# The second feed-forward block as two passes over DRAM instead of one fused loop per half of the tokens

## The chip, the cores and the metric

The kernel runs on one core of one Trainium2 chip. The metric is the device time of one execution in microseconds. Three runs of the kernel before took 2210.45, 2212.99 and 2214.95 us; the median is 2212.99 us.

## The reference

One inference step of a one-layer trunk, over 1104 columns of tokens (16 meta tokens, 1024 prompt tokens, 64 sample tokens), with 1024 features and 2816 hidden features, in fp32:

```
x = x + 0.5 * SwiGLU_1(RMSNorm(x))
x = x + W_out @ concat[RG-LRU, mLSTM, GLA](W_in @ RMSNorm(x))
x = x + 0.5 * SwiGLU_2(RMSNorm(x))
y = RMSNorm_final(x)            # the meta tokens are dropped here

def swiglu(x, w1, w3, w2):
    return (silu(x @ w1) * (x @ w3)) @ w2
```

The change lies in the third line and the last one: SwiGLU_2 on the 1088 columns that are put out (the meta tokens' 16 are not needed there), and the final norm.

## The kernel before

Tokens lie along the free dimension and features along the partitions (128 at a time, so D = 8 blocks and the hidden layer 22, `NFB`). Every fp32 product is made of three matmuls of a reduced type: `split` (L111) casts a tensor to its high part on ScalarE and subtracts that on VectorE to get the low part, and PE then sums hi·hi, hi·lo and lo·hi. So each weight that comes from DRAM costs ScalarE a cast and VectorE a subtraction (`whi`, `wlo`) before PE can use it.

The products with w1 and w3 are made of half-size blocks by a scheme with seven products in place of eight (`seven`, L1400): the weights' four blocks are combined on GpSimd (`ws`, L1384, four operations for each 256 features) into seven left operands, the normalized tokens' four blocks on VectorE into seven right operands `op1` to `op7` (L1344), each split; then 7 x 12 matmuls of half the part's width, and VectorE and ScalarE add the partial results from PSUM into `c` (L1416, L1420, L1424).

The second feed-forward block (L1270 to L1608) works on two parts of the tokens, `PARTS`: 576 columns (half width 288) and 512 columns (half width 256). For each part it goes through eleven groups of 256 hidden features (`f0`), and for each group does all of this:

- `weights` for w1 (two loads of 512 KB, four combinations, seven splits), `seven`, and the same for w3;
- `halves` (L1434): two loads of 512 KB of w2, each split (`w2h`, `w2l`);
- the gate (L1579 to L1581: tanh on ScalarE, two VectorE operations) and a split of its result (`hh`, `hl`);
- `gemm2` (L1525): 8 blocks of outputs, each 6 matmuls into PSUM per column block, which VectorE adds into the residual `X` (L1538), at every group.

w1, w3 and w2 are so loaded and prepared once for each part, which is 44 calls of `weights` and 44 halves of w2. The operands of part 1 are made while part 0 runs: squares at group 4, `norms` at 6, the normalization spread over groups 8 to 14, and the split operands in part 0's last group, into the buffers of part 0. The unnormalized part 1 waits in DRAM meanwhile (`xback`) and is loaded again. The outputs of part 0 (transposition of 4 blocks at a time into PSUM, L1451, a copy by ScalarE, squares, `rsq`, scaling, store) are spread over part 1's groups 4 to 12. The last group of part 1 has a form of its own (L1588 to L1603): its columns are transposed ahead, the w2 products are made with tokens on the partitions, and each chunk of 128 tokens is normed and stored as soon as it is summed.

Ahead of all this stands `wout2` (L1486): the last third of the mixer's output projection, eight blocks of 24 matmuls, interleaved with the squares, the norm and the operands of part 0.

The order of the instructions on each engine comes from a list scheduler of the framework: the program's order with priorities, and `tc.high_priority` around part 0's preparation. Loads and stores are issued by SP's queue, in that queue's order.

Names: `wraw` is a raw w1, w3 or w_out tile, `w` a raw w2 tile, `rb` the broadcast norm factor, `acc` and `sq` the squares, `rsv`, `rsa`, `rsy` the small tiles of the reciprocal square root, `xt` an output tile, `xps` its PSUM tile.

Of the kernel before, what the change touches and what calls it, by code (L numbers as in the profile page):

```python
# [30 lines left out]
PARTS = [(288, [(0, 64), (64, 128), (192, 128), (320, 128), (448, 128)]), (256, [(0, 128), (128, 128), (256, 128), (384, 128)])]  # L31
# [5 lines left out]
def tile_step(ctx, tc, A, O):  # L37
# [1233 lines left out]
    with ExitStack() as ph:  # L1271

        def pool(name, bufs=1, **kw):
            return ph.enter_context(tc.tile_pool(name=name, bufs=bufs, reuse_waits="tile", **kw))

        xp, wq, op_, tp, bp = pool("x3"), pool("w3"), pool("o3"), pool("t3", 2), pool("b3", 2)
        pq, pz = pool("q3", 2, space=PSUM), pool("z3", 2, space=PSUM)

# [6 lines left out]


        X = [xp.tile([128, 8, 2 * n], F32, tag=f"x{i}", name=f"x{i}") for i, (n, _) in enumerate(PARTS)]
        xback = tc.dram_tile([128, 8, 512], F32, name="xback")

        def load0():  # L1290
            nc.sync.dma_start(X[0][:, :, 0:320], xdr2[0][:, :, 16:336])
            nc.sync.dma_start(X[0][:, :, 320:576], xdr2[1][:, :, 0:256])


        def squares(i):
            n = PARTS[i][0]
            acc = tp.tile([128, 576], F32, tag="acc", name="acc", bufs=1)[:, : 2 * n]
            S.activation(acc, X[i][:, 0, :], AF.Square)
            for k in range(1, 8):
                q = tp.tile([128, 576], F32, tag="h", name="sq", bufs=3)[:, : 2 * n]  # L1300
                S.activation(q, X[i][:, k, :], AF.Square)
                V.tensor_tensor(acc, acc, q, OP.add)
            return acc

        def norms(i, acc):
            n = PARTS[i][0]
            r = tp.tile([128, 2, 288], F32, tag="rb", name="rb", bufs=1)[:, :, :n]
# [12 lines left out]
            for h in range(2):  # L1320
                q = pz_("rbp")
                for j, (hh, o, m) in enumerate(cs):
                    if hh == h:
                        d = tp.tile([128, 128], F32, tag="dg", name="dg", bufs=3)
# [6 lines left out]
        def normal(i, r, ks):  # L1331
            n = PARTS[i][0]
            for k in ks:
# [5 lines left out]
        def blocks(i):  # L1339
            n = PARTS[i][0]  # L1340
            return [X[i][:, 4 * fh : 4 * fh + 4, th * n : th * n + n] for fh, th in ((0, 0), (0, 1), (1, 0), (1, 1))]

        def minus(out, x, y):
            V.tensor_tensor(out, x, y, OP.subtract)  # L1344

        def temp(i):
            return bp.tile([128, 4, 288], F32, tag="bf", name="bf")[:, :, : PARTS[i][0]]

        def differences(i):
            b11, b12, b21, b22 = blocks(i)  # L1350
            t1, t2 = temp(i), temp(i)
            minus(t1, b12, b11)
            minus(t2, b22, t1)
            minus(b12, b22, b12)
            return t1, t2

        def operands(i, ts):
            n = PARTS[i][0]
            b11, t3, b21, b22 = blocks(i)
            t1, t2 = ts  # L1360
            ops = {}
            for p, x in zip(ORDER, (b11, t2, b21, t3, t1, t2, b22)):
                if p == 4:
                    minus(t2, b21, t2)
                t = op_.tile([128, 2, 4, 288], F32R, tag=f"op{p}", name=f"op{p}")
                ops[p] = (t[:, 0, :, :n], t[:, 1, :, :n])
                split(*ops[p], x)
            return ops
# [3 lines left out]
        def weights(w, f):  # L1372
            r = []
            for i in range(2):
                t = wq.tile([128, 4, 256], F32, tag="raw", name="wraw", bufs=4)
# [24 lines left out]
        def seven(u, ops, n, y1, y2):  # L1400
            a, b, c = bank("a"), bank("b"), bank("c")
            s = tp.tile([128, 288], F32, tag="p1", name="p1")[:, :n]
# [31 lines left out]
        def halves(f0):  # L1434
            wr = A["ffn2_w2"][f0 * 128 : f0 * 128 + 256, :].rearrange("(g p) (i c) -> i p g c", g=2, i=2)
            out = []
            for i in range(2):
                raw = lp.tile([128, 2, 512], F32, tag="w2", name="w2", bufs=1)
                lo = lp.tile([128, 2, 512], F32R, tag="w2l", name="w2l", bufs=2)
                hi = lp.tile([128, 2, 512], F32R, tag="w2h", name="w2h", bufs=2)  # L1440
                nc.sync.dma_start(raw, wr[i])
                split(hi, lo, raw)
                out.append((hi, lo))
            return out


        def turned(x, i, o, m):
            for q in range(2):
                p = pz_("xps").rearrange("p (k t) -> p k t", k=4)
                for k in range(4):  # L1450
                    PE.transpose(p[:m, k, :], X[i][:, 4 * q + k, o : o + m], ident)  # L1451
                S.copy(x[:m, q * 512 : q * 512 + 512].rearrange("p (k t) -> p k t", k=4), p[:m])

        def output(i, j, o, m, x, add=None):
            ahead = add is not None
            ss = tp.tile([128, 2], F32, tag="ssf", name="ssf", bufs=RB)[:m]
            v = tp.tile([128, 8], F32, tag="rsv", name="rsv", bufs=RB)[:m, :1]
            for q in range(2):
                xq = x[:m, q * 512 : q * 512 + 512]
                if add:  # L1460
                    add(q, xq)
# [199 lines left out]
```

## Time and profile before

| | before |
|---|---|
| median of three runs | 2212.99 us |
| the profiled execution: its time | 2212.36 us |
| its span (first to last instruction) | 2210.6 us |
| PE busy | 2112.8 us, 96%, 13758 matmuls |
| VectorE (DVE) busy | 1533.3 us, 69% |
| ScalarE (ACT) busy | 846.7 us, 38% |
| GpSimd (POOL) busy | 342.7 us, 16% |
| DMA | 195.90 MB, mean 89 GB/s |

The span is what the trace covers; the execution's time is 1.8 us longer, for what lies around it. Every later row is read against the span. A matmul's record overlaps the next one's, so PE's pace is read from the starts of successive matmuls, not from their durations. The granted clock of PE over the whole execution is 0.985 of full speed.

### The profile page before, as it was taken

Reading aid. Unit: us, or ns where it says so; the run is one execution under the profiler, and the core shown is the slowest. Engines: PE = TensorE matmul, PEld = TensorE weight load, DVE = VectorE, ACT = ScalarE, POOL = GpSimd, SP = SyncE. Lnnn points to the kernel's source line nnn. Section 1 sums busy time; section 2 is a strip of 40 time slices with the busy share of each in tenths; the row PEclk is TensorE's granted clock in tenths of the full one; section 3 lists DMA queues with packets and bytes.
Section 4 is the critical chain, followed back from the end, with each engine's and each line's share of the span. In section 5 each row is a group of like instructions: output and inputs, shape, how many; then the busy total and the mean of one; then the engine's idle time right before and its main releaser. Section 6 shows DMA issues by size and latency. Waiting matters only on the chain.

```text
span 2210.6 us, 35427 instructions
## 1 busy us (share of the span) xinstructions
PE 2112.8 (96%) x13758; PEld 2032.8 (92%) x13758; DVE 1533.3 (69%) x3214; ACT 846.7 (38%) x1672; POOL 342.7 (16%) x321
## 2 busy tenths in 40 slices
PE   8999999999999999999998897799999989999997
PEld 7999999999999999978997797799999989888896
DVE  7444545454444467766787885998978798779896
ACT  6221111111111144645646753444434344435543
POOL 3000000000000021000000000343333233234331
PEclk9999999999999999999999999999999999999999
DMA  6011111111111125544434337533233233233421
GB/s 180 29 48 39 53 34 48 48 48 39 48 48 39 39 73 152 131 141 132 111 100 105 87 101 211 173 90 96 77 89 93 86 115 92 90 101 96 124 87 48
DMA packets 237500, 195.90 MB, mean 89 GB/s; under 512 B 41887, under 2 KB 216516, under 8 KB 236820
## 3 DMA queue, kind: packets, MB, share of 16 engines
q1 hardware_dynamic: 232540, 191.86, 29.5%
q10 hardware_dynamic: 4792, 1.78, 0.4%
q8 instruction: 108, 1.77, 0.3%
q14 instruction: 60, 0.49, 0.1%
HBM read 162.28 MB, written 31.32 MB: 88 GB/s over the span
## 4 chain that ended last, share of the span: by engine, by line
PE 77%; DVE 13%; DMA 4%; ACT 3%; issue 2%; SPq 0%; DVEq 0%; ACTq 0%
PE p L196 24%; PE p L245 11%; PE p L1535 9%; PE pw L196 8%; PE b L1409 7%; PE c L1409 4%; PE a L1409 4%; DVE wlo L113 3%; PE pwo L196 2%; PE pA L752 1%; DVE c L1416 1%; PE pq L550 1%; DMA wraw<-in_w_out_dram 1%; DVE sl L134 1%; DVE h L1580 1%
## 5 line engine op out<-in xcount | busy, mean ns | idle before, releaser
L112 ACT CAST whi<-wraw 128x512 fp32r<-128x512 f32 (+1 forms) x242 | 189.7, 787 | 338.0 <-PE p L245 116.4
L113 DVE TENSOR_TENSOR wlo<-wraw,whi 128x512 fp32r<-128x512 f32 (+1 forms) x242 | 242.6, 1004 | 32.4 <-ACT whi L112 28.6
L247 DVE SCALAR_TENSOR_TENSOR x<-p,x 128x384 f32<-128x384 f32 (+1 forms) x264 | 139.6, 539 | 153.7 <-PE p L245 153.1
L196 PE MATMUL p<-sh,whi 128*128 128x384 f32 (+1 forms) x1056 | 205.0, 331 | 0.4 <-ACT sh L133 0.4
L196 PE MATMUL p<-sl,whi 128*128 128x384 f32 (+1 forms) x1056 | 203.2, 329 | 0.0
L196 PE MATMUL p<-sh,wlo 128*128 128x384 f32 (+1 forms) x1056 | 201.9, 329 | 0.0
L112 ACT CAST whi<-ws 128x512 fp32r<-128x512 f32 x176 | 108.9, 620 | 193.2 <-PE b L1409 117.9
L1384 POOL TENSOR_TENSOR ws<-wraw 128x512 f32<-128x512 f32 x88 | 137.5, 1563 | 290.3 <-DVE wlo L113 197.0
L196 PEld LDWEIGHTS p<-sh,whi 128*128 128x128 f32 x1056 | 179.4, 189 | 1.6 <-ACT sh L133 1.4
L196 PEld LDWEIGHTS p<-sh,wlo 128*128 128x128 f32 x1056 | 180.7, 188 | 0.0
L196 PEld LDWEIGHTS p<-sl,whi 128*128 128x128 f32 x1056 | 179.7, 188 | 0.1
L112 ACT CAST hh<-h 128x384 fp32r<-128x384 f32 (+3 forms) x110 | 61.5, 559 | 302.3 <-DVE h L229 278.2
L245 PE MATMUL p<-hh,whi 128*128 128x384 f32 (+1 forms) x528 | 174.3, 330 | 1.9 <-DVE x L247 1.8
L1535 PE MATMUL p<-hh,w2h 128*128 128x288 f32 (+1 forms) x512 | 166.1, 332 | 10.0 <-DVE x L1538 9.7
L1409 PE MATMUL b<-op,whi 128*128 128x288 f32 (+1 forms) x1056 | 164.5, 293 | 11.5 <-DVE c L1416 9.7
L1538 DVE SCALAR_TENSOR_TENSOR x<-p,x 128x288 f32<-128x288 f32 (+1 forms) x256 | 131.2, 523 | 62.8 <-PE p L1535 61.9
L245 PE MATMUL p<-hh,wlo 128*128 128x384 f32 (+1 forms) x528 | 174.1, 330 | 0.0
L245 PE MATMUL p<-hl,whi 128*128 128x384 f32 (+1 forms) x528 | 173.5, 329 | 0.0
L1535 PE MATMUL p<-hl,w2h 128*128 128x288 f32 (+1 forms) x512 | 168.1, 329 | 0.6 <-DVE hl L113 0.6
L1535 PE MATMUL p<-hh,w2l 128*128 128x288 f32 (+1 forms) x512 | 167.6, 328 | 0.0
L1409 PEld LDWEIGHTS b<-op,whi 128*128 128x128 f32 x1056 | 147.5, 192 | 15.7 <-DVE c L1416 12.0
L148 POOL TENSOR_TENSOR acc<-acc,sq 128x384 f32<-128x384 f32 (+1 forms) x21 | 22.8, 1085 | 773.7 <-ACT sq L147 773.1
(467 smaller groups left out, 4570.3 us busy)
## 6 DMA issues: line engine op xcount, KB each, us to landing
wraw<-in_ffn_w_dram SPq DMA_DIRECT2D x154, 512.0 KB
w<-in_ffn_w_dram SPq DMA_DIRECT2D x44, 512.0 KB
wraw<-in_w_in_dram SPq DMA_DIRECT2D x16, 512.0 KB
wraw<-in_w_out_dram SPq DMA_DIRECT2D x16, 512.0 KB
out_y_prompt_dram<-xt SPq DMA_DIRECT2D x16, 256.0 KB
xspill<-x SPq DMA_DIRECT2D x2, 1536.0 KB
sl<-in_x_prompt_dram SPq DMA_DIRECT2D x5, 512.0 KB
x<-xspill SPq DMA_DIRECT2D x2, 1280.0 KB
```

The lines of the kernel that those rows point to most:

```text
L112: S.copy(hi, x)
L113: V.tensor_tensor(lo, x, hi.bitcast(F32), OP.subtract)
L134: V.scalar_tensor_tensor(lo[:, k, :n], X[:, k, :n], vc(gname, k), hi[:, k, :n].bitcast(F32), OP.mult, OP.subtract)
L148: G.tensor_tensor(sums[b], sums[b], s, OP.add)
L196: PE.matmul(p, wsl(ww, k), xsl(xx, k), start=i == 0, stop=i == tot - 1)
L245: PE.matmul(p[:, :n], w[:, g, :], x[:, :n], start=i == 0, stop=i == 3 * GRP - 1)
L247: V.scalar_tensor_tensor(X[b][:, d, :n], p[:, :n], 0.25, X[b][:, d, :n], OP.mult, OP.add)
L550: PE.matmul(p[:96, h, :m], wt[:, kb, sl, 0:96], cm[:, kb, :m], start=i == 0, stop=i == len(ks) - 1)
L1384: G.tensor_tensor(t, x, y, op)
L1409: PE.matmul(t[:, :n], ww[:, k, :], xx[:, k, :], start=first and i == 0, stop=i == 11, skip_group_check=True,)
L1535: PE.matmul(p[:, :m], w[:, g, :], x, start=c == 0, stop=c == 5)
L1538: V.scalar_tensor_tensor(xs, p[:, :m], 0.25, xs, OP.mult, OP.add)
```

## The change

The second feed-forward block becomes two phases.

**Phase 1.** The split operands of both parts are resident in SBUF at once (`oa`, `ob`), so that `weights` is called once for a group of 256 features and both parts are multiplied with it. Groups 0 and 2 (`SOLO`) run for part 0 alone at first, while part 1 is loaded, normed and split; they run again for part 1 at the end. That makes 2 x (2 + 9 + 2) = 26 calls of `weights`. The gated result is not split there but stored, as fp32, to a DRAM tensor `hidden`. The raw weight buffers go from four to three. In `wout2` each block of the residual is now loaded, added to and stored again (`xw`).

**Phase 2.** Three thirds of the tokens (320, 384 and 384 columns). For each, `hidden` is loaded in 22 tiles (`hr`, three buffers) and split; w2 is streamed as 16 tiles of six or five feature blocks by 256 outputs (`w2`, two buffers) and split; the products over all 22 feature blocks are summed in PSUM, so that a third has 8 additions into the residual tile `xo`. The outputs of a third follow the next third's products; those of the last two thirds come after the last product. The special form of the last group, `xback` and its reload are gone.

The core of the diff:

```
+THIRDS = [(320, 0, ..., -64), (384, 320, ..., 256), (384, 704, ..., 640)]
+KQ = [(0, 6), (6, 6), (12, 5), (17, 5)]
+SOLO = (0, 2)
...
+        def group(f0, parts):
+            for nm in ("1", "3"):
+                u = weights(A["ffn2_w" + nm], f0)
+                for i in parts:
...
+                    seven(u, ops[i], n, *ys_[nm, i])
+                    if nm == "3":
+                        for g in range(2):
+                            y1, y3 = ys_["1", i][g], ys_["3", i][g]
+                            h = htile("h")[:, : 2 * n]
+                            S.activation(h, y1, AF.Tanh, scale=0.5)
+                            V.scalar_tensor_tensor(h, h, 1.0, y1, OP.add, OP.mult)
+                            V.tensor_tensor(h, h, y3, OP.mult)
+                            nc.sync.dma_start(hd[:, f0 + g, c0 : c0 + 2 * n], h)
...
+        for f0 in SOLO:
+            group(f0, (0,))
+            if f0 == 0:
+                xload(1)
+                acc = squares(1)
+                r = norms(1, acc)
+                normal(1, r)
+                ops[1] = operands(1, ob)
+        for f0 in range(0, NFB, 2):
+            if f0 not in SOLO:
+                group(f0, (0, 1))
...
+        for f0 in SOLO:
+            group(f0, (1,))
...
+        def third(j):
+            x = tp.tile([128, 8, 384], F32, tag="xo", name="xo", bufs=2)[:, :, :n]
+            nc.sync.dma_start(x, xdr2[j][:, :, 16:336] if j == 0 else xdr2[j])
...
+            for d in range(0, 8, 2):
+                for k0, nk in KQ:
...
+                    nc.sync.dma_start(t[0], wr[:, k0 : k0 + nk, d * 128 : d * 128 + 256])
+                    split(t[1], t[2], t[0])
...
+                for e in range(2):
+                    V.scalar_tensor_tensor(x[:, d + e, :], ps_[e], 0.25, x[:, d + e, :], OP.mult, OP.add)
...
+        xs = [third(0)]
+        for j in range(1, 3):
+            xs.append(third(j))
+            outputs(j - 1, xs[j - 1])
+        outputs(2, xs[2])
```

Up to the end of the mixer the orders of all engines are the same in both programs. Three places after that are shown, as each engine is given its work.

First, VectorE of the change, where part 1's operands become ready (`op_14266` is the first of them; `dg` feeds the broadcast of the norm factor, `x<-x,vec,rb` is the normalization):

```order
L1344 TENSOR_SCALAR dg<-ident,rsy 128x128 x4
L1469 SCALAR_TENSOR_TENSOR h<-h,c 128x576 x2
L1470 TENSOR_TENSOR h<-h,c 128x576
L1353 SCALAR_TENSOR_TENSOR x<-x,vec,rb 128x512 x8
L1432 TENSOR_TENSOR c<-p_14621,b 128x288
L1470 TENSOR_TENSOR h<-h,c 128x576
L122 TENSOR_TENSOR op_14266<-x,op_14266 128x1024
L122 TENSOR_TENSOR op_14275<-x,op_14275 128x1024
```

In the kernel before, the same normalization stands in rows of four and three operations among the groups of part 0, and the first split of part 1 in part 0's last group; now all of it stands together behind the first two groups.

Second, SP's queue of the change from the end of phase 1 into the first third (`w_19663` and the like are tiles of w2, `xo` the residual, `gb` the final norm's factor):

```order
L1393 DMA wraw<-in_ffn_w_dram 128x4x256 x2
L1472 DMA hidden<-h 128x512 x3
L1534 DMA hr<-hidden 128x320 x2
L1472 DMA hidden<-h 128x512
L1534 DMA hr<-hidden 128x320
L1570 DMA w_19663<-in_ffn_w_dram 128x6x256
...
L1550 DMA xo<-xspill_1_85 128x3072
L1570 DMA w_19747<-in_ffn_w_dram 128x5x256
L1570 DMA w_19783<-in_ffn_w_dram 128x5x256
L1534 DMA hr<-hidden 128x320 x3
L1570 DMA w_19823<-in_ffn_w_dram 128x6x256
L1534 DMA hr<-hidden 128x320 x11
```

The kernel before has no such place: its queue alternates `wraw` and `w` loads up to the last group. Here every load of phase 2 stands behind the last but one or the last store of `hidden`.

Third, the end of PE's queue, before:

```order
L1409 MATMUL c<-op_18587,wlo 128x256 x4
L1451 MATMUL xps<-ident,x_13481 128x128 x32
L1599 MATMUL p_22923<-w2h,hh 128x512
L1599 MATMUL p_22923<-w2h,hl 128x512
L1599 MATMUL p_22923<-w2l,hh 128x512
```

and in the change:

```order
L1576 MATMUL p_21735<-h_21223,w2l 128x384
L1576 MATMUL p_21735<-h_21236,w2l 128x384 x3
L1576 MATMUL p_21735<-h_21249,w2l 128x384
L1596 MATMUL xps<-ident,xo 128x128 x48
L1662 UNCONDITIONAL_BRANCH
```

Before, the last 32 transposes stand ahead of the last products; now 48 stand behind them.

## Rows read from the trace of the kernel before

**Rows 1.** Busy time by stretch: us; busy us (instructions) PE, PEld, DVE, ACT, POOL; PEclk, DMA share, GB/s.

```profile
400.00:800.00 400.00, 400.00 (x2393) 400.00 (x2392) 192.85 (x329) 70.75 (x103) 0.00 (x0) 1.00 0.15 44
1350.00:1360.00 10.00, 0.60 (x2) 0.60 (x3) 0.62 (x2) 1.14 (x2) 0.00 (x0) 0.61 1.11 342
1401.00:1500.00 99.00, 90.72 (x649) 87.75 (x648) 98.80 (x132) 50.12 (x84) 42.99 (x26) 1.00 0.41 131
1500.00:2100.00 600.00, 574.61 (x4147) 554.28 (x4146) 502.29 (x843) 252.30 (x440) 202.04 (x135) 0.98 0.32 96
2100.00:2198.00 98.00, 95.46 (x616) 85.21 (x615) 81.27 (x144) 40.63 (x75) 25.85 (x19) 1.00 0.18 55
```

**Rows 2.** Timeline of PE: start us, us from first start to last end, instruction, count [idle].

```profile
1359.40 2.93 PE L1502 MATMUL pwo<-sh,whi 128*128 128x384 f32 x8 [12.01 <-ACT whi L112]
...
1402.05 1.55 PE L1502 MATMUL pwo<-sh,wlo 128*128 128x384 f32 x8
1403.44 1.22 PE L1409 MATMUL a<-op,whi 128*128 128x288 f32 x8
1404.49 0.69 PE L1409 MATMUL a<-op,wlo 128*128 128x288 f32 x4
```

**Rows 3.** Groups by form, 1397 to 2211 us: count | busy us, mean ns | idle before.

```profile
L113 DVE TENSOR_TENSOR wlo<-ws,whi 128x512 fp32r<-128x512 f32 x176 | 138.0, 788 | 5.1 <-ACT whi L112 4.1 <-PE b L1409 0.5
L113 DVE TENSOR_TENSOR wlo<-wraw,whi 128x512 fp32r<-128x512 f32 x131 | 116.1, 886 | 7.3 <-ACT whi L112 7.0
L1416 DVE TENSOR_TENSOR c<-p,b 128x288 f32<-128x288 f32 x66 | 29.3, 444 | 7.9 <-PE b L1409 7.6
L1580 DVE SCALAR_TENSOR_TENSOR h<-h,c 128x576 f32<-128x576 f32 x22 | 24.6, 1127 | 0.2
L1581 DVE TENSOR_TENSOR h<-h,c 128x576 f32<-128x576 f32 x22 | 18.7, 854 | 0.0
L1335 DVE SCALAR_TENSOR_TENSOR x<-x,vec,rb 128x512 f32<-128x512 f32 x8 | 6.5, 859 | 0.0
L113 DVE TENSOR_TENSOR op<-x,op 128x1152 fp32r<-128x1152 f32 x4 | 5.4, 1347 | 0.0
L113 DVE TENSOR_TENSOR op<-bf,op 128x1152 fp32r<-128x1152 f32 x3 | 5.1, 1709 | 0.0
L1451 PE MATMUL xps<-ident,x 128*128 128x128 f32 x64 | 9.4, 278 | 1.1 <-ACT xt L1452 1.1
L1463 ACT ACTIVATE sqf<-xt 128x512 f32<-128x512 f32 x16 | 10.1, 632 | 9.8 <-DVE xt L1601 4.7 <-DVE rsa L122 2.5 <-DVE rsa L121 2.4
L1478 DVE SCALAR_TENSOR_TENSOR xt<-xt,rsy,gb 128x512 f32<-128x512 f32 x8 | 5.6, 740 | 0.0
```

**Rows 4.** Groups by form, whole span: the split of a 384-column tile in the first block.

```profile
L112 ACT CAST hh<-h 128x384 fp32r<-128x384 f32 x44 | 22.6, 514 | 136.2 <-DVE h L229 136.2
...
L113 DVE TENSOR_TENSOR hl<-h,hh 128x384 fp32r<-128x384 f32 x44 | 24.7, 561 | 17.4 <-ACT hh L112 17.4
```

**Rows 5.** The chain that ended last: loads of small tiles that had been stored to DRAM.

```profile
1179.23 3.00 DMA zg<-z_z
...
1239.11 3.63 DMA qk<-z_qk
```

**Rows 6.** Timeline: a subtraction, small VectorE operations, POOL beside one, PE's last matmul.

```profile
1388.09 0.17 DVE L121 TENSOR_TENSOR rsa<-rsy 128x6 f32<-128x6 f32 x1
1388.29 0.17 DVE L122 SCALAR_TENSOR_TENSOR rsa<-rsa,rsv 128x6 f32<-128x6 f32 x1
...
1401.31 0.68 DVE L113 TENSOR_TENSOR wlo<-ws,whi 128x512 fp32r<-128x512 f32 x1
...
2194.57 1.28 POOL L1465 TENSOR_TENSOR xt<-xt,gb 128x512 f32<-128x512 f32 x1
...
2194.66 1.21 DVE L122 SCALAR_TENSOR_TENSOR rsa<-rsa,rsv 128x1 f32<-128x1 f32 x1
...
2198.04 0.39 PE L1599 MATMUL p<-w2l,hh 128*128 128x512 f32 x1
```

More of the change, by code (lines that the diff above doesn't have):

```diff
@@ L1271, in tile_step, with pool @@
     with ExitStack() as ph:
[L1273 to L1277, printed above, removed]
+        def pool(st, name, bufs=1, **kw):
+            return st.enter_context(tc.tile_pool(name=name, bufs=bufs, reuse_waits="tile", **kw))
+        oa = pool(ph, "oa3")
+        p1st = ExitStack()
+        xp, bp, wq, tp, cp = (pool(p1st, n) for n in ("x3", "b3", "w3", "t3", "c3"))
+        pq, pz = pool(p1st, "q3", 2, space=PSUM), pool(p1st, "z3", 2, space=PSUM)
         def bank(tag):
@@ L1328, in norms, with normal, operands, put @@
             return r
-        def normal(i, r, ks):
-            n = PARTS[i][0]
-            for k in ks:
+        def normal(i, r):
+            for k in range(8):
                 x = X[i][:, k, :].rearrange("p (h t) -> p h t", h=2)
                 V.scalar_tensor_tensor(x, x, vc("ffn2_norm_g", k), r, OP.mult, OP.mult)
-        def blocks(i):
+        def operands(i, pool):
             n = PARTS[i][0]
[L1341 to L1353, printed above, removed]
-            minus(b12, b22, b12)
[L1355 to L1367, printed above, removed]
+            b11, b12, b21, b22 = [
+                X[i][:, 4 * fh : 4 * fh + 4, th * n : th * n + n] for fh, th in ((0, 0), (0, 1), (1, 0), (1, 1))
+            ]
+            ops = {}
+            def put(p, x):
+                t = pool.tile([128, 2, 4, n], F32R, tag=f"op{i}{p}", name=f"op{i}{p}")
+                ops[p] = (t[:, 0], t[:, 1])
+                split(*ops[p], x)
+            def minus(out, x, y):
+                V.tensor_tensor(out, x, y, OP.subtract)
+            put(1, b11)
+            minus(b11, b12, b11)
+            t2 = bp.tile([128, 4, 288], F32, tag="bf", name="bf")[:, :, :n]
+            minus(t2, b22, b11)
+            put(6, t2)
+            put(2, b21)
+            minus(b12, b22, b12)
+            put(7, b12)
+            put(5, b11)
+            minus(t2, b21, t2)
+            put(4, t2)
+            put(3, b22)
             return ops
@@ L1432, in seven @@
             add(y1[:, h2], y1[:, h2], c)
[L1434 to L1444, printed above, removed]
@@ L1511, in tile_step @@
             acc = squares(0)
[L1512 removed]
+            r = norms(0, acc)
         wout2(range(5, 8))
         with tc.high_priority(offset=W2):
[L1515 to L1518 removed]
+            normal(0, r)
+            ops[0] = operands(0, oa)
         late.close()
[L1520 to L1522 removed]
@@ new lines, in tile_step, with hidden @@
+        ob = pool(p1st, "ob3", side="right")
+        for f0 in SOLO:
[9 more added lines that the diff above has]
+                group(f0, (0, 1))
+        def hidden(j, tile, per):
+            n, c0 = THIRDS[j][:2]
+            hs, t = [], None
+            for k in range(NFB):
+                pair = []
+                for c in range(2):
+                    if (2 * k + c) % per == 0:
+                        t = tile((2 * k + c) // per)
+                    pair.append(t[:, (2 * k + c) % per, :])
+                raw = hp.tile([128, 384], F32, tag="hr", name="hr", bufs=3)[:, :n]
+                nc.sync.dma_start(raw, hd[:, k, c0 : c0 + n])
+                split(*pair, raw)
+                hs.append(pair)
+            return hs
```

227 lines of the change are left out of this document (90 added, 137 removed), and 3 rows, old and new, of the table THIRDS.

## The prediction, made before the change was run

> **What bounds the kernel now.** I read the page's busy shares first, then busy time by stretch, then PE's timeline for its pace, then the groups by form for what VectorE does. PE is busy nearly throughout, so the time is PE's floor plus what PE loses. In the first feed-forward block PE loses nothing, with VectorE busy 193 of 400 us. In the stage that changes VectorE is busy 98.8 of 99 us at first and 502 of 600 later, and PE is idle for 8.3, 25.4 and 2.5 us of the three stretches, 36.2 in all [rows 1].
>
> PE's pace is the distance between starts: 1.39 us for 8 matmuls of 384 columns (0.1735 each), 1.05 for 8 of 288 (0.131) [rows 2]. Both are 0.00045 us a column, which gives 0.117 at 256, 0.145 at 320 and 0.231 at 512. The floor of the stage: the seven-product scheme is 22 x 84 = 1848 matmuls of each width, 1848 x (0.131 + 0.117) = 458.3 us; w2 is 1056 x 0.131 + 528 x 0.231 = 260.3; 72 transposes at 9.4/64 = 0.147 [rows 3] are 10.6. Sum 729.2. The first product starts at 1403.4 [rows 2], the last matmul ends at 2198.3 [rows 6]; less 24 matmuls of w_out in between (4.2 us) that is 790.7 us. So **61.5 us are lost**: 36.2 idle, the rest matmuls below the fastest pace. That is the most that the change can win here. Behind the last matmul 12.3 us remain to the span's end at 2210.6.
>
> **The change part by part.**
>
> *PE's work* stays: the scheme keeps its 458.3 us, w2 becomes 528 x 0.145 + 1056 x 0.1735 = 259.8, and 48 of the transposes leave the stage for the tail, 24 x 0.147 = 3.5 remain. Floor 721.6.
>
> *Preparation and sums removed.* 18 of 44 weight sets go, each 7 subtractions of 0.79 or 0.89 us [rows 3], some 105 us of VectorE; 232 of 256 additions into the residual go too. None is on PE's path by itself; their worth is the 61.5 us, and no more.
>
> *Start.* The first split of part 0 no longer stands behind a block subtraction of 1.35 us (nearest row: the splits of the same size [rows 3]), and the first w_out tiles no longer queue behind the load of part 1, whose wait shows as 12.0 us of idle PE [rows 2]. Most of that idle has other causes; I take 3.4 us together, ends 0 and 6. The first product starts at 1400.0.
>
> *Opening.* Between the first split of part 0 and the first of part 1, VectorE's order holds 30 weight subtractions (24.9 us, at 0.79 and 0.89), 7 operand splits (4 x 1.35 + 3 x 1.71 = 10.5), 4 block subtractions (5.4 at 1.35), 21 sums (9.3 at 0.444), 8 gate operations (7.9 at 1.13 and 0.85), 7 sums of squares (6.0, taken like the normalization's 0.86), the norm's small operations (3.5), the normalization (8 x 0.859 = 6.9) and two more (1.8): 76 us [rows 3]. PE has 4.2 + 384 x 0.131 = 54.5 us to do before it needs part 1. It waits for the difference, **21 us**. Ends: 30 subtractions at 0.68, the single one seen [rows 6], give 16, less 2 for overlap: 14; 25 if the load of part 1 is late.
>
> *Rest of phase 1.* A group of both parts costs VectorE 14 subtractions (11.6), 20 sums (8.6), 8 gate operations (7.3), 27.5 us beside 336 matmuls of 41.7: 66%, between the 48% at which nothing is lost and the 84% at which 4% is idle [rows 1]. I take 2 us for nine groups. The two groups at the end for part 1 alone have 19 us of VectorE beside 19.7 of PE, as full as the stretch that lost 8 in 99 [rows 1]: 5 us. Together **7**, ends 3 and 14. The 44 stores of the hidden tiles hold up nothing but SP, whose weight loads run three tiles ahead.
>
> *Transition.* All loads of phase 2 stand behind the last stores of phase 1 on SP. Up to the ninth hidden tile the queue holds 9 tiles (1.5 MB), four w2 tiles (2.9 MB), the final norm's factor and two residuals (2.9 and 0.5 MB): 7.6 MB, 22 us at the 342 GB/s of the fullest stretch [rows 1]. The other 13 hidden tiles then pass through three buffers: a load of 3.0 to 3.6 us [rows 5], a cast of 0.51, a subtraction of 0.56 [rows 4], 4.1 us for three or 1.37 each: 18 us. The last one is ready some 43 us after the store and 46 us after PE's last product of phase 1, while PE has 132 x 0.145 = 19 us of work with them. It loses **26 us**. Ends: 13, if only the volume counts (10 MB), 36 if the third w2 tile's wait, queued ahead of eleven hidden loads, adds as much again as a third of it. The first matmuls after 12 us of idle took 2.93 us in place of 1.39 [rows 2], half the clock; such restarts and other slow stretches cost 5, ends 0 and 10.
>
> The Trainium skill ("DMA: Bandwidth & Descriptors", section "Bandwidth") would batch transfers to at least 1 MiB, which speaks against 66 loads of 164 to 197 KB; its section "Anatomy of one DMA" prices one at about 2.0 us plus bytes over 436 GB/s, by which a hidden tile would be an estimated 2.4 us, where the rows have 3.0 and more. By it the 13 tiles cost an estimated 15 us and the forecast would be 3 lower.
>
> *Rest of phase 2.* A w2 tile feeds 36 matmuls, 5.2 to 6.2 us, and its split is about three times a 512-column one on either engine. With two buffers it keeps up: **3**, ends 0 and 12.
>
> *Tail.* The 48 transposes, the copies, squares and norms of six chunks come behind the last product. ScalarE: 12 copies and 12 squares at 0.63 [rows 3], some 17 us with their accumulator reads. VectorE per chunk: 13 small operations, 0.20 apart [rows 6], and two scalings of 0.74 [rows 3], 4.1 us. In the order given, a chunk's norm follows its squares and the chunks go one behind the other on VectorE: 0.5 + 2.8 for the first chunk's transposes and ScalarE, 6 x 4.1, 3.0 for the last store (like the loads of rows 5): **31 us** against 12.3. Ends: 25, if ScalarE alone sets the pace, and 34.
>
> I take 0.20 and not more for the small operations since no GpSimd work is left there: the 1.21 us one ran beside a GpSimd multiplication of 1.28 [rows 6]. The Trainium skill ("SBUF — State Buffer", section "SBUF: two separate sides") says that GpSimd and VectorE lock a shared pair of ports in turn and that the loser waits for the whole instruction; by that rule too the tail has none of these waits, and with them, two a chunk, it would be an estimated 12 us longer.
>
> **Sum.** 1400.0 + 4.2 + 721.6 = 2125.8; losses 21 + 7 + 26 + 5 + 3 = 62 bring the last product to 2187.8; the tail to a span of 2218.8. The execution adds 1.8 (2212.36 against 2210.6) and the median of the runs lies 0.6 above that execution, which I leave out: 2220.6, less 1.5 for two of the losses overlapping (the clock's restart lies partly in the transition's wait): **2219 us**. So the lost 61.5 us are lost again elsewhere, and the longer tail decides.
>
> **The rivals.**
>
> *Loads overlap better, faster.* Hidden tiles whose loads overlap in flight come at the volume's pace: the transition costs 13, the opening 16, the tail 29: 2219 - 13 - 5 - 2 = 2199. It decides when a hidden tile takes under 0.8 us in the mean. For it: 342 GB/s is reached [rows 1]. Against it: three buffers and a split behind each load. Chance 0.31.
>
> *ScalarE paces the tail, no change.* If the norms of neighbouring chunks interleave on VectorE, the tail is 25: 2213. Against it: VectorE takes its instructions in order. Chance 0.16.
>
> *w2 tiles late throughout, slower.* SP takes its queue in order, so a w2 load stands behind hidden loads that wait for a split. If each of the 32 tiles of the first two thirds comes 0.8 us late, that is 25 more: 2244. It decides when a tile's load takes longer than the 5 to 6 us that PE needs for one tile. Against it: 16 MB in each 77 to 92 us, 173 to 205 GB/s, is well below 342. Chance 0.13.
>
> **How the numbers follow.** The forecast case, 2219, has 0.40; its own range is 2208 to 2232. A difference of 0.2% (4.4 us) is what the runs can tell from none. Of the forecast's 0.40, 0.32 lies above 2217.4 and 0.08 within the band: slower 0.32 + 0.13 = 0.45, same 0.08 + 0.16 = 0.24, faster 0.31. All low ends together would give some 2180, all high ends 2260; leaving a tenth out at each side, 2194 to 2244.
>
> **What would show it.** After: an idle PE of some 20 us where part 1's first product stands, behind VectorE's splits; near 1890 us a stall of 20 to 35 us behind hidden loads or their splits; PE nearly gapless after that; the last w2 matmul near 2188 and 31 us behind it. The forecast is wrong if the stall at the transition is under 15 us, if PE still loses 4% in the nine shared groups, or if the tail is under 26 us.

## The result and the profile after

The changed kernel takes 2229.07 us (median of four runs, 2227.24 to 2232.44), the kernel before, on the same chip, 2211.72. The ratio is 1.008 with a 95% interval of 1.006 to 1.010: slower, as forecast, and 10 us above the 2219 us of the forecast, inside its range. The profiled execution took 2232.44 us, the highest of the four, with a span of 2230.7; its stages below are read against that.

The page of the changed kernel, busy time and three rows of the 40 slices (tenths of a slice):

```profile
PE 2111.1 (95%) x13758; PEld 2056.1 (92%) x13758; DVE 1350.9 (61%) x2878; ACT 797.3 (36%) x1568; POOL 217.0 (10%) x241
...
PE   8999999999999999999998896789999999599996
...
DVE  7554544444444577766777884897656658465434
...
PEclk9999999999999999999999998889999999799998
```

In the kernel before, PE's slices were

```profile
PE   8999999999999999999998897799999989999997
```

PE has the same 13758 matmuls. VectorE sheds 182 us, GpSimd 126. One slice of PE falls far, the 35th, where the phases meet (9 to 5); the 25th, the 27th and the last fall by one step. The stretches of the changed kernel (columns as in [rows 1]):

```profile
1413.00:1500.00 87.00, 69.01 (x444) 64.02 (x445) 84.41 (x114) 39.08 (x64) 31.39 (x19) 0.91 0.31 102
1500.00:1909.00 409.00, 408.49 (x3288) 407.97 (x3287) 275.57 (x432) 142.71 (x269) 116.75 (x80) 1.00 0.24 77
...
1909.00:1960.00 51.00, 28.23 (x150) 25.84 (x149) 20.32 (x31) 17.18 (x29) 0.00 (x0) 0.77 0.76 247
1960.00:2200.00 240.00, 239.69 (x1452) 239.26 (x1451) 110.79 (x154) 85.19 (x104) 0.00 (x0) 1.00 0.53 172
```

This is the answer to [rows 1]. Over 649 of the stage's some 800 us PE is idle for 0.8 us; the 36 us of idle time spread over the stage before are gone. They are back in two lumps: 18.0 us idle in the opening (VectorE 84.4 of 87 busy) and 22.8 where the phases meet (VectorE 20 of 51 busy, so not VectorE's doing). And the end is longer, the timeline of the changed kernel's tail (columns as in [rows 2]):

```profile
2203.07 3.52 PE L1596 MATMUL xps<-ident,xo 128*128 128x128 f32 x28
...
2210.30 17.04 SPq L1607 DMA_DIRECT2D out_y_prompt_dram<-xt  x12
...
2213.11 1.07 ACT L1597 COPY xt<-xps 128x512 f32<-128x512 f32 x2 [2.72 <-DMA out_y_prompt_dram<-xt]
...
2216.57 1.07 ACT L1597 COPY xt<-xps 128x512 f32<-128x512 f32 x2 [1.15 <-DMA out_y_prompt_dram<-xt]
```

From the first transposition behind the last product (2203.1) to the end are 27.6 us, against 12.3 before. The fourth and fifth chunk wait for an output tile's store, since there are three such tiles.

What was not foreseen lies ahead of the stage. SP's queue and PE's first products, in the changed kernel:

```profile
1352.14 0.59 SPq L1488 DMA_DIRECT2D xw<-xspill  x1
1357.82 0.53 SPq L1305 DMA_DIRECT2D x<-xspill  x1
1358.40 15.71 SPq L1480 DMA_DIRECT2D wraw<-in_w_out_dram  x7
...
1366.12 2.93 PE L1493 MATMUL pwo<-sh,whi 128*128 128x384 f32 x8 [15.77 <-ACT whi L121]
...
1413.72 0.80 PE L1425 MATMUL a<-op,whi 128*128 128x288 f32 x4 [1.13 <-ACT op L121]
```

and SP's in the kernel before:

```profile
1349.18 9.35 SPq L1491 DMA_DIRECT2D wraw<-in_w_out_dram  x4
1358.63 1.68 SPq L1292 DMA_DIRECT2D x<-xspill  x1
```

Before, four w_out tiles go out ahead of the second half of part 0's load, which has to wait for the mixer's last store. Now all of them stand behind it, and SP waits 5.0 us at that load (from 1352.7 to 1357.8). PE's idle time there grows from 12.0 to 15.8 us, and the first product of the stage comes at 1413.7 in place of 1403.4 [rows 2]. Of these 10.3 us, 3.0 come from the mixer, which the change does not touch: its last product starts at 1347.1 us in the trace before, at 1350.0 in the changed kernel's, and anywhere from 1345.4 to 1354.2 in the traces of this study.

The order in SP's queue accounts for the 3.8 us of longer idle time, not for all of the other 7.3. From the first w_out product to the first product of the stage it is 47.6 us in place of 44.0. In that stretch PE waits longer for the broadcast of part 0's norm, first in the changed kernel, then before:

```profile
1398.84 2.96 PE L1345 MATMUL rbp<-dg,ones 128*128 128x128 f32 x10 [7.72 <-DVE dg L1344]
```

```profile
1390.23 3.50 PE L1326 MATMUL rbp<-dg,ones 128*128 128x128 f32 x12 [5.76 <-DVE dg L1325]
```

Of the eleven small VectorE operations ahead of it, four took 1.1 to 1.2 us in the changed kernel and two before, 2.0 us more; these ran beside GpSimd's operations (last section). No run moved GpSimd's work away from there, so this part is read from the traces alone.

In what follows a **loss** is the time between starts of successive matmuls beyond the pace of their width (0.1325 us at 288 columns, 0.118 at 256, 0.147 at 320, 0.1735 at 384), summed over a stretch; it holds slow matmuls as well as gaps, so it is larger than the idle time where the granted clock is below 1 (0.91 in the opening, 0.77 where the phases meet). For the changed kernel: 28.9 us in the opening (to 1505 us), under 0.5 in the rest of phase 1, 29.5 where the phases meet, none after that.

### The profile page after: what moved, and what is told of

Read it like the earlier page. It is cut to its first block, busy times and chain, and to the rows that moved or that the text cites. A ratio compares the mean times of both kernels' runs of the same rounds, so it can differ in the third digit from the quotient of the medians.

```text
span 2230.7 us, 35007 instructions
## 1 busy us (share of the span) xinstructions
PE 2111.1 (95%) x13758; PEld 2056.1 (92%) x13758; DVE 1350.9 (61%) x2878; ACT 797.3 (36%) x1568; POOL 217.0 (10%) x241
## 4 chain that ended last, share of the span: by engine, by line
PE 84%; DVE 7%; DMA 5%; ACT 3%; issue 1%; SPq 0%; DVEq 0%; ACTq 0%
PE p L205 23%; PE p L254 11%; PE p L1576 10%; PE pw L205 9%; PE b L1425 8%; PE c L1425 5%; PE a L1425 5%; PE pwo L205 2%; PE pwo L1493 2%; DMA hr<-hidden 1%; PE pq L559 1%; PE pA L761 1%; DVE sl L143 1%; DMA w<-in_ffn_w_dram 1%; DVE wlo L122 1%
## 5 line engine op out<-in xcount | busy, mean ns | idle before, releaser
L121 ACT CAST whi<-wraw 128x1024 fp32r<-128x1024 f32 (+1 forms) x188 | 156.4, 834 | 324.2 <-PE p L254 116.4
L1576 PE MATMUL p<-h,w2h 128*128 128x384 f32 (+1 forms) x1056 | 195.5, 332 | 23.1 <-ACT h L121 12.0
L122 DVE TENSOR_TENSOR wlo<-wraw,whi 128x1024 fp32r<-128x1024 f32 (+1 forms) x188 | 186.1, 992 | 35.4 <-ACT whi L121 26.4
L1576 PEld LDWEIGHTS p<-h,w2h 128*128 128x128 f32 x1056 | 179.9, 193 | 25.7 <-ACT h L121 13.8
L122 DVE TENSOR_TENSOR w2l<-w,w2h 128x1536 fp32r<-128x1536 f32 (+1 forms) x48 | 77.9, 1625 | 104.9 <-ACT w2h L121 104.2
L121 ACT CAST hh<-h 128x384 fp32r<-128x384 f32 (+1 forms) x66 | 33.0, 500 | 278.2 <-DVE h L238 278.2
L1425 PE MATMUL a<-op,whi 128*128 128x256 f32 (+1 forms) x704 | 105.4, 290 | 7.6 <-ACT op L121 6.9
L121 ACT CAST w2h<-w 128x1536 fp32r<-128x1536 f32 (+1 forms) x48 | 65.9, 1372 | 127.7 <-PE p L1576 112.6
L1400 POOL TENSOR_TENSOR ws<-wraw 128x512 f32<-128x512 f32 x52 | 77.9, 1498 | 303.7 <-DVE wlo L122 206.6
L1425 PE MATMUL c<-op,whi 128*128 128x256 f32 (+1 forms) x704 | 104.2, 287 | 1.0 <-DVE c L1432 0.6
```

The costliest lines, as they stand in the source:

```text
L121: S.copy(hi, x)
L122: V.tensor_tensor(lo, x, hi.bitcast(F32), OP.subtract)
L1400: G.tensor_tensor(t, x, y, op)
L1425: PE.matmul(t[:, :n], ww[:, k, :], xx[:, k, :], start=first and i == 0, stop=i == 11, skip_group_check=True,)
L1576: PE.matmul(ps_[e], t[a][:, k, e * 128 : e * 128 + 128], hs[k0 + k][b], start=k0 == 0 and i == 0, stop=k0 + nk == NFB and i == 3 * nk - 1, ...
```

## The experiments

All ratios are to the kernel before, run beside each; the changed kernel's is 1.008.

| run | edit to the changed kernel | ratio (95%) | what moved in the trace |
|---|---|---|---|
| e1 | w_out loads first | 1.0057 (1.0042 to 1.0072) | idle before w_out 15.8 to 10.6 |
| e2 | residual loads held | 1.0091 (1.0074 to 1.0109) | loss at the meeting 29.5 to 29.1 |
| e3 | five hidden buffers | 1.0069 (1.0054 to 1.0084) | 29.5 to 25.4 |
| e4 | outputs spread | 1.0060 (1.0043 to 1.0076) | tail 27.6 to 17.8 |
| e5 | squares summed on PE | 1.0090 (1.0072 to 1.0108) | opening 28.9 to 29.1 |
| e6 | phase 2 loads early | 1.0007 (0.9996 to 1.0017) | 29.5 to 6.7, last groups lose 5 |
| e8 | nothing shared | 1.0191 (1.0172 to 1.0209) | rest of phase 1: 0 to 25.9 |
| e7 | e1, e4, e5, e6 | 0.9958 (0.9943 to 0.9973) | idle before w_out 10.6, tail 17.3 |
| e9 | opening without sums | one run, 2221.66 us, no interval | opening 28.9 to 20.9 |
| e12 | subtractions on GpSimd | 1.0102 (1.0086 to 1.0117) | opening 28.9 to 27.1 |
| e10 | e1, e4, e6 | 0.9949 (0.9936 to 0.9961) | idle before w_out 10.4, tail 17.3 |
| e13 | e10, tail copies on VectorE | 0.9938 (0.9924 to 0.9952) | tail 17.3 to 16.0 |

By their times, only e6, e8 and the combined runs e7, e10 and e13 differ from the changed kernel (its interval is 1.006 to 1.010); what the other edits did is read from one trace each. The edits are shown shortened, with comments added.

**e1, the start.**

```
-        xload(0)                      # both halves
-        wout2(range(0, 5))
+        xload(0)                      # first half
+        wout2(range(0, 2))
+        nc.sync.dma_start(X[0][:, :, 320:576], xdr2[1][:, :, 0:256])
+        wout2(range(2, 5))
```

> The changed kernel, with the second half of part 0's load issued behind the first two w_out blocks' loads. In the changed kernel SP reaches the w_out tiles only at 1358.4 us, behind that load, which waited 5.7 us for the mixer's last store (issued 1352.1, next issue 1357.8); before the change they went out at 1349.2. Theory (SP's order delays the stage's start): PE's first w_out product of the stage moves from 1366.1 to about 1360, and the kernel is 5 to 7 us faster than the changed one, near 2223. Rival (the tiles' data could not come earlier, the DMA engines being full there): the first product stays within 1.5 us of 1366 and the time within 2 us of 2229.

SP's queue and PE in that run:

```profile
1348.31 2.02 SPq L1479 DMA_DIRECT2D wraw<-in_w_out_dram  x2
1353.25 0.53 SPq L1500 DMA_DIRECT2D x<-xspill  x1
...
1356.25 2.93 PE L1492 MATMUL pwo<-sh,whi 128*128 128x384 f32 x8 [10.56 <-ACT whi L121]
```

The wait of SP still takes 3 us, but two tiles are ahead of it, and PE's idle time falls by 5.2 us, below that of the kernel before. (PE's first w_out product came 9.9 us earlier in the trace; 4.7 of that is the mixer, which ended earlier in this execution.) The order in SP's queue was the cause of that wait. The ratio falls by 0.0023, 5 us, which the intervals do not separate from none.

**e2 and e3, the meeting of the phases: volume or round trips.** In e2 the loads of `xo` and `gb` wait for a tiny copy that depends on a hidden tile:

```
-            nc.sync.dma_start(x, xdr2[j][:, :, 16:336] if j == 0 else xdr2[j])
...
+            # first[0]: a column of hidden tile 15 of third 0, then of tile 21
+            V.tensor_copy(x[:, 0, 0:1], first[0].bitcast(F32))
+            nc.sync.dma_start(x, xdr2[j][:, :, 16:336] if j == 0 else xdr2[j])
```

and in e3 the hidden tiles get more buffers:

```
-                raw = hp.tile([128, 384], F32, tag="hr", name="hr", bufs=3)[:, :n]
+                raw = hp.tile([128, 384], F32, tag="hr", name="hr", bufs=5)[:, :n]
```

> The changed kernel, with the loads of the residual tiles and of the final norm's factor held until hidden tiles 15 and 21 of the first third are split, so that 3.4 MB leave the queue ahead of the hidden tiles; one tiny VectorE copy each holds them. Theory A (volume and queue order make the stall at the phase change): the 29.5 us that PE loses between 1909 and 1960 us fall by up to 10, to about 20, time near 2220. Theory B (round trips of the hidden tiles through three buffers make it): the loss falls by less than 4 us.

> The changed kernel with five buffers for raw hidden tiles in place of three. Theory B (round trips of the hidden tiles): a hidden tile then costs some 0.85 us in place of 1.37 (six times 4.2 us for five), so the loss of 29.5 us at the phase change falls by 6 or more, time near 2222. Theory A (volume and queue order): falls by less than 3 us.

Neither theory came through: the loss fell by 0.4 us in e2, where A wanted up to 10, and by 4.1 in e3, where B wanted 6 or more. The chains of the two runs say why. In e2, with the volume gone, the chain goes through the hidden tiles one after the other:

```profile
1944.32 4.78 DMA hr<-hidden
1949.12 0.47 ACT h L121
1949.61 0.50 DVE h L122
...
1953.39 5.40 DMA hr<-hidden
```

In e3, with more buffers, it goes through the large loads:

```profile
1914.24 10.96 DMA xo<-xspill
...
1925.26 10.05 DMA w<-in_ffn_w_dram
```

Both were there; each hid the other's removal. And neither edit touched PE's first and longest wait, which is for the first w2 tile, asked for only when phase 1 ends. In the changed kernel, in e2 and in e3:

```profile
1920.48 1.97 PE L1576 MATMUL p<-h,w2h 128*128 128x320 f32 x6 [10.54 <-ACT w2h L121]
```

```profile
1922.06 1.97 PE L1585 MATMUL p<-h,w2h 128*128 128x320 f32 x6 [10.64 <-ACT w2h L121]
```

```profile
1921.73 3.03 PE L1576 MATMUL p<-h,w2h 128*128 128x320 f32 x10 [11.97 <-ACT w2h L121]
```

What all three have in common is that nothing could start before phase 1 ended.

**e6, that common cause.** The raw tiles of phase 2 go into the space of the normalized tokens, dead since the opening, and the first third's hidden tiles are loaded ahead of the last two groups.

```
-        xp, bp, wq, tp, cp = (pool(p1st, n) for n in ("x3", "b3", "w3", "t3", "c3"))
+        xp = pool(ph, "x3")
+        bp, wq, tp, cp = (pool(p1st, n) for n in ("b3", "w3", "t3", "c3"))
...
+        region = xp.tile([128, 8, 576], F32, tag="x", name="region")   # 2 raw w2, 4 raw hidden tiles
+        hs0 = hidden(0, ...)
         for f0 in SOLO:
             group(f0, (1,))
```

> The changed kernel, with the raw w2 and hidden tiles of phase 2 in the space of the normalized tokens, which is free after the opening, and the loads and splits of the first third's hidden tiles ahead of the last two groups in the program, since that third lies in part 0, whose hidden tiles are complete by then. Theory C (the stall at the phase change is there because phase 2's buffers lie in phase 1's space and become free with its end, so that everything starts at once): PE's 29.5 us of loss fall to 6 or less, the last two groups, where VectorE then has 51 us of work beside 39 of PE, lose 8 to 12, and the kernel is 12 to 18 us faster than the changed one, near 2214. Theory B (three buffers' round trips): four buffers here, so the total loss of the last two groups and the phase change falls by 4 to 6 only. Theory A (volume): no gain, the same bytes in the same stretch.

Theory C holds. PE at the meeting, and the last two groups and the first quarter of the third:

```profile
1912.82 0.63 PE L1426 MATMUL c<-op,wlo 128*128 128x256 f32 x4
1913.29 3.69 PE L1584 MATMUL p<-h,w2h 128*128 128x320 f32 x24
...
1928.72 4.73 PE L1584 MATMUL p<-h,w2h 128*128 128x320 f32 x20 [4.70 <-ACT w2h L121]
```

```profile
1860.00:1912.00 52.00, 46.85 (x387) 45.54 (x387) 47.63 (x74) 28.89 (x58) 19.38 (x12) 1.00 0.38 115
1912.00:1960.00 48.00, 43.30 (x287) 42.83 (x286) 26.76 (x34) 17.12 (x24) 0.00 (x0) 0.96 0.85 287
```

The first product of phase 2 follows the last of phase 1 without a gap. One wait of 4.7 us for the third w2 tile is left, and the last groups lose 5 us, half of what was expected: VectorE has more room there than the means of [rows 3] gave. In the changed kernel's own last groups, where I had set 19 us of VectorE beside 19.7 of PE, PE lost under 1. Ratio 1.0007, 16 us faster than the changed kernel. The edit changes two things, where phase 2's raw tiles lie and how early the first third's hidden tiles are asked for; how much each is worth was not tested.

**e4, the tail.** Each chunk of outputs is issued behind a pair of output blocks of the next third.

```
+                if d // 2 < len(after):
+                    outputs(*after[d // 2])
...
-            xs.append(third(j))
-            outputs(j - 1, xs[j - 1])
+            xs.append(third(j, [(j - 1, xs[j - 1], [c]) for c in range(3)]))
```

> The changed kernel with each third's three output chunks issued behind the first three pairs of output blocks of the next third, so that 24 transposes stand behind the last product in place of 48. Theory (the tail is paced by the chunks behind the last product, some 4 us each on VectorE and the buffers): the stretch from the last w2 product to the end falls from 27.6 us to 15 to 17, PE gains about 3.5 us of transposes ahead of it, time near 2220 to 2221. Rival (the spread transposes make PE wait for PSUM or the copies in the third): the end of the last product moves later by over 6 us and the gain is under 6.

Three chunks less behind the last product take 9.8 us off the tail (17.8 left, where 15 to 17 were expected). The 24 transposes more ahead of it take 2.3 us of PE, and phase 2 as a whole, first product to last, grows by 1.4 (282.4 to 283.8). That is some 8 us net in the trace; the ratio falls by 0.0020, 4.4 us, with intervals wide enough for either.

**e8, one part undone.** No weight set serves both parts.

```
-SOLO = (0, 2)
+SOLO = tuple(range(0, 22, 2))
```

> The changed kernel, with no group shared: all eleven groups for part 0, then all eleven for part 1, so that w1 and w3 are prepared twice again as before the change (44 weight sets, 92% VectorE in phase 1 by the means), with all else of the change kept. Theory S (sharing the weights is what frees phase 1 of its losses): phase 1 loses 4% again, 15 to 20 us, less 18 that the opening gains since part 1 is not needed for 240 us: time within 4 us of the changed kernel. Theory E (what freed phase 1 is that w2's sums and splits left it): phase 1 loses under 6 us, the opening loses 10 to 14 in place of 28.9, and the kernel is 10 to 15 us faster than the changed one.

The stretches of that run:

```profile
1411.00:1500.00 89.00, 74.79 (x504) 69.84 (x504) 87.49 (x119) 43.78 (x75) 37.59 (x22) 0.97 0.36 111
1500.00:1700.00 200.00, 190.24 (x1384) 188.68 (x1385) 188.45 (x249) 97.00 (x173) 111.51 (x67) 0.97 0.37 111
1700.00:1930.00 230.00, 221.80 (x1844) 217.78 (x1843) 224.08 (x304) 113.83 (x213) 132.52 (x83) 1.00 0.39 118
```

Theory S: VectorE is full again and the rest of phase 1 loses 25.9 us, more than the 15 to 20 expected. So the shared weights are what the change gains, 24 us of the time by the medians' ratios. The opening did not gain 18 us as expected: PE had all of part 0 to do, needed nothing of part 1, and yet lost 25.3 us up to 1505. That points to VectorE, which has part 1's norm and operands in its list ahead of the next weights.

**e5, e9, e12, what bounds the opening.** e5 sums the squares of part 1 by one-column products, e9 leaves seven of the eight out, e12 gives two of seven weight subtractions in part 0's first groups to GpSimd:

```
# e5: in place of V.tensor_tensor(acc, acc, q, OP.add) and the products of acc
+                for j, (h, o, m) in enumerate(cs):
+                    PE.matmul(ss[:m, j : j + 1], q[:, h * n + o : h * n + o + m], ones[:, :1], ...)
# e9
-                acc = squares(1)
+                S.activation(acc, X[1][:, 0, :], AF.Square)
# e12, in weights(), for two of the seven operands
-                split(hi, lo, x)
+                S.copy(hi, x)
+                G.tensor_tensor(lo, x, hi.bitcast(F32), OP.subtract)
```

> The changed kernel, with part 1's eight squares summed by PE (32 products of one column, the first norm's own way of summing across partitions) in place of seven VectorE additions, 0.68 to 1.77 us each in the changed kernel's trace, some 8 us in all. Theory (VectorE's instruction list bounds the opening): PE's first product with part 1 comes 5 to 8 us earlier, the loss there falls from 28.9 to 21 to 24 us, time near 2223. Rival (the load of part 1 or ScalarE bounds it): the loss falls by less than 2 us.

> The changed kernel, leaving out seven of the eight squares of part 1 and their seven VectorE additions (6.9 us in the changed kernel's trace), so that part 1's norm is that of its first feature block only; nothing takes their place on PE. Theory (VectorE's instruction list bounds the opening; in the run with the sums on PE, PE's one-column products took the place of the additions): PE's first product with part 1 comes 6 to 8 us earlier after its first product than the 80.5 us of the changed kernel, and its loss in the opening falls from 28.9 to 21 to 23 us. Rival (the load of part 1, 2 MB issued only when the operands of part 0 are split, and what follows it in series): the additions stand in that series too, so the gain would be the same or up to 9 us with the squares' waits; if the gain is under 3, both are wrong and the order of PE's queue is the limit.

> The changed kernel, with two of the seven weight subtractions of each weight set of groups 0 and 2 of part 0 (8 subtractions in all) on GpSimd in place of VectorE. They are not in the series load, squares, norm, normalization. Theory (VectorE's list): VectorE sheds 8 x 0.7 to 0.9 = 6 us, the opening's loss of 28.9 falls by 3 to 6. Rival (the series): under 2 us. Third (GpSimd's operations hold up VectorE's, as the 1.1 to 1.7 us that small and 512-column operations take beside them suggest): the loss grows by 2 or more.

e5: VectorE's busy time in 90 us falls from 87.4 to 77.6, but PE's 64 one-column matmuls took 10.2 us and stood in the series themselves, and the squares waited for buffers that hold hidden tiles until they are stored. No gain. e9: without the sums and with nothing in their place, part 1's first product comes 69.2 us after part 0's in place of 80.5, 11.3 us earlier where 6 to 8 were expected; the loss is 20.9. e12: the trace shows that nothing was taken off VectorE. The weight subtractions in that run, 1410 to 1500 us, and then in the changed kernel, 1412 to 1502 us:

```profile
L122 DVE TENSOR_TENSOR wlo<-ws,whi 128x512 fp32r<-128x512 f32 x19 | 19.6, 1041 | 0.0
...
L1413 POOL TENSOR_TENSOR wlo<-wraw,whi 128x512 fp32r<-128x512 f32 x7 | 13.1, 1869 | 8.0 <-ACT whi L1412 6.5 <-PE pwo L1497 1.5
...
L122 DVE TENSOR_TENSOR wlo<-wraw,whi 128x512 fp32r<-128x512 f32 x6 | 7.0, 1169 | 0.0
```

```profile
L122 DVE TENSOR_TENSOR wlo<-ws,whi 128x512 fp32r<-128x512 f32 x19 | 14.4, 764 | 0.0
L122 DVE TENSOR_TENSOR wlo<-wraw,whi 128x512 fp32r<-128x512 f32 x15 | 12.7, 849 | 0.0
```

25 subtractions now take 26.6 us where 34 took 27.1. Ten of the 25 ran beside a GpSimd operation and took 1.2 to 1.8 us, the other 15 took 0.68; three of the ten stood beside one of GpSimd's subtractions, the rest beside its combinations. So e12 did not test what it was meant to. The opening is a loss of 28.9 us in a stretch in which VectorE is full (e8 and the changed kernel), and work taken out of it comes back (e9); how much of it is VectorE's list and how much the series load, squares, norm, normalization stays open, since e9 shortens both.

**e7, e10, e13, the repairs together.**

> The changed kernel with four edits together: the w_out loads ahead of the second half of part 0's load, the outputs of each third spread over the next, part 1's squares on PE, and the early loads of phase 2. If the losses add up as independent stretches (theory): 10 (start, by the spans of the first run) + 6 (tail, less the transposes) + 5 (opening) + 15 (phase change) us less than the changed kernel, near 2192, and so faster than the kernel before by 0.6 to 1.0%. Rival (a repair in one stretch uncovers the next wait, VectorE in the last groups above all): less than half of the 36 us, not faster than the kernel before.

> The three edits that each moved their own stretch, without the squares on PE: w_out loads first, outputs spread, early loads of phase 2. If the squares on PE were worth nothing, it comes within 3 us of the run with four edits (ratio 0.9958 to the kernel before); if PE's one-column products cost it PE time, 3 to 6 us faster, ratio 0.993 to 0.995.

> The three repairs, with the copies of the last third's six transposed half tiles out of PSUM on VectorE in place of ScalarE. In the run with three repairs VectorE has nothing to do for the first 3.8 us of the tail while ScalarE does copies and squares, 8.7 us in all. Theory (ScalarE paces the tail up to its last square): VectorE's first norm starts 1.5 to 2 us earlier and the stretch behind the last product falls from 17.6 to 15 to 16, 2 us in all, ratio to the kernel before 0.0005 to 0.001 lower than 0.9949, which the intervals hardly tell; the trace decides. Rival (VectorE's three norms in a row pace it): 0 to 1 us later, since the copies now stand in its order too.

e7 came out 9 us above its expectation: of its 36 us, the start gave 5 and not 10 (the mixer's part was no gain) and the opening nothing. e10, without the squares on PE, is at 0.9949, 2 us below e7 and within its interval: the squares on PE were worth nothing. The changed kernel's 1.008 less the single effects of e1, e4 and e6 (0.0023, 0.0020, 0.0073) gives 0.9964, so the repairs add up within the intervals. e13 moves the last third's copies:

```
-                    S.copy(x[:, h].rearrange("p (k t) -> p k t", k=4), p[:m])
+                    if j == 2:
+                        V.tensor_copy(x[:, h].rearrange("p (k t) -> p k t", k=4), p[:m])
```

Its transposes begin, in PE's timeline, at

```profile
2179.25 2.81 PE L1607 MATMUL xps<-ident,xo 128*128 128x128 f32 x24
```

and the span ends at 2195.2: 16.0 us, against 17.3 in e10 (2180.6 to 2197.9). The tail is where the edit was to act; in time e13 and e10 are not told apart. e13 has the lowest ratio, 2196.98 us, 0.6% below the kernel before and 1.4% below the changed one.

## Why the prediction was right, and where its terms were not

The forecast was that the 61.5 us lost before are lost again elsewhere and the longer tail decides. That is what the trace shows, with the sum 13 us short of the profiled execution (2219 against 2232.4) and 10 short of the median. None of its three signs of being wrong came: PE is idle for 22.8 us where the phases meet, for 0.5 of 409 in the rest of phase 1, and the tail is 27.6. That the sum came so near is in part luck, since terms that were too small (start, opening, pace) and terms that were too large (rest of phase 1, restarts and rest of phase 2, tail) offset each other.

- **Preparation removed, none of it on PE's path by itself**: right. PE loses nothing over 649 us, and for the 409 of phase 1 e8 shows that the sharing is the reason, 24 us.
- **Start, -3.4 us, ends 0 and 6: the step that failed.** Measured +7.3 beside the mixer's 3.0. I credited the change with w_out tiles no longer behind part 1's load and did not look at what they stood behind instead. The load of part 0's second half stood ahead of them in the order of SP's queue, and it waits for a store. e1 takes 5.2 us off PE's idle time there, 15.8 to 10.6. The rest, 3.6 us between the first w_out product and the first product, is in part the longer wait for part 0's norm, for which the prediction had no term.
- **Opening, 21 us, ends 14 and 25**: 28.9, outside. VectorE's 76 us were right: its first split of part 0 begins at 1419.0, its first of part 1 at 1496.7, as the changed kernel's timeline shows:

```profile
1418.96 4.98 DVE L122 TENSOR_TENSOR op<-x,op 128x1152 fp32r<-128x1152 f32 x3
...
1496.68 3.49 DVE L122 TENSOR_TENSOR op<-x,op 128x1024 fp32r<-128x1024 f32 x3
```

  But I set PE's first product beside it at the same moment; it needs only the cast of ScalarE and came 5 us earlier, so PE ran out of work that much sooner. 80.5 us lie between PE's first products with the two parts, and 54.5 of work; 3 more are lost up to 1505. What I did not see is that VectorE, whose list is the measure here, sits idle just ahead of part 0's normalization:

```profile
1407.83 0.69 DVE L122 TENSOR_TENSOR wlo<-ws,whi 128x512 fp32r<-128x512 f32 x1 [6.21 <-PE pwo L1493]
```

  The normalization starts right behind this one, at 1408.4. Before, VectorE waited 1.9 us there. No run tried to fill these 6.2 us.
- **Rest of phase 1, 7 us**: 0.5. I priced the groups for part 1 alone like the stretch before the change that lost 8 in 99, at the same fullness of VectorE. In a stretch of 44 us in these groups VectorE was busy for 39, as I had set, and PE idle for 0.5, so the fullness alone did not give the loss:

```profile
1865.00:1909.00 44.00, 43.49 (x370) 43.13 (x369) 38.95 (x58) 19.91 (x37) 17.55 (x12) 1.00 0.23 73
```

- **Transition, 26 us and some for the clock**: 29.5, right in size, in mechanism only in part. The sum put the volume (7.6 MB; its parts add up to 7.8) and the round trips one behind the other; by e2 and e3 they run side by side. PE's waits in it were one of 10.5 us for the first w2 tile and five, 12.0 us in all, for hidden tiles. A hidden tile's load took 2.2 to 6.6 us in the three chains (14 loads), where [rows 5] had 3.0 to 3.6. By the Trainium skill ("DMA: Bandwidth & Descriptors", "Anatomy of one DMA"), whose formula there is for DMAs issued from GpSimd, it would be an estimated 2.4 us. Three of the loads here, which are issued from SP, took 2.2 us; the longest ones, 4.5 to 6.6, stood right behind a w2 tile or a residual in SP's queue, and the measured ones decide.
- **Rest of phase 2, 3 us**: none. **Tail, 31 us**: 27.6. The rival that norms of neighbouring chunks interleave on VectorE was partly right (they do), but three output tiles and their stores then set the start of the fourth and fifth chunk.
- **Pace**: 0.131 and 0.117 us were read from 8 matmuls; over the stage they are 0.1325 and 0.118, 5 us more of floor in both kernels.

By terms, from the forecast to the profiled execution: mixer +3.0, start +10.7, opening +7.9, rest of phase 1 -6.5, transition +1.5 (with 2 of the 5 us for restarts counted to it), rest of phase 2 and the other 3 us for restarts -6, floor +4.6, tail -3.4, the overlap that I took off +1.5: +13.3.

## What to carry to other kernels

When a fused loop becomes two phases, the place to look at is where they meet: what the second phase needs must have buffers of its own before the first one ends, or every load, cast and split starts at once; here that was worth as much as two thirds of the change's own gain (16 of 24 us). Two causes that run side by side hide each other's removal, so a test that removes one and moves nothing refutes neither. And a change to what is loaded has to be followed through the order of the queue up to the next load that waits for a store.

## What the runs showed of the hardware

Some of VectorE's smallest operations took about seven times as long beside GpSimd, 1.1 to 1.2 us in place of 0.17. VectorE and GpSimd in the changed kernel, in the norm of part 0 (timeline: start us, us):

```profile
1393.72 1.11 DVE L130 TENSOR_TENSOR rsa<-rsy 128x6 f32<-128x6 f32 x1
1394.86 1.19 DVE L131 SCALAR_TENSOR_TENSOR rsa<-rsa,rsv 128x6 f32<-128x6 f32 x1
...
1397.30 0.17 DVE L130 TENSOR_TENSOR rsa<-rsy 128x6 f32<-128x6 f32 x1
```

```profile
1393.53 1.27 POOL L1400 TENSOR_TENSOR ws<-ws,wraw 128x512 f32<-128x512 f32 x1
1394.77 1.25 POOL L1400 TENSOR_TENSOR ws<-wraw 128x512 f32<-128x512 f32 x1
1395.99 1.26 POOL L1400 TENSOR_TENSOR ws<-wraw,ws 128x512 f32<-128x512 f32 x1
```

Each slow one ends as a GpSimd operation ends (1394.8, 1396.0); the same operation takes 0.17 us once GpSimd is done (1397.25). This agrees with the Trainium skill ("SBUF — State Buffer", "SBUF: two separate sides"), by which the two engines hold a shared pair of ports in turn for a whole instruction, and with e12, where VectorE's subtractions beside a GpSimd operation took 1.2 to 1.8 us and the others 0.68. In the tail, without GpSimd, the small operations took 0.15 to 0.16 us, as the forecast assumed.
